# Attention scores of two heads on the two halves of TensorE's rows, three products each, in place of stacked pairs of products; instruction and buffer tables redrawn

## The chip, the cores and the metric

The kernel runs on one core of a Trainium2 chip. The metric is the device time of one execution in microseconds (us); the time before is the median of three runs. Times inside a run come from one profiled execution. The engines are TensorE (PE, with its weight loads shown apart as PEld), VectorE (DVE), ScalarE (ACT), GpSimd (POOL) and SyncE (SP, which here issues transfers).

## The reference

One decoder layer on 512 tokens of width 1024, all in float32: a normalised input is projected to the queries, keys and values of three token mixers and to their gates; the mixers' outputs are gated, added, projected and normalised; a gated feed-forward part follows. The change concerns the scores of two of the mixers (head width 64):

```python
# sliding window with sinks: 8 query heads share 2 key heads, blocks of 128
scores = jnp.einsum('bnqhgd,bnkhd->bnhgqk', qb, kband).astype(jnp.float32) * (d ** -0.5)
scores = jnp.where(mask[None, :, None, None], scores + bias[None, None], -jnp.inf)
...
# stick-breaking: 8 heads, block i of 128 queries against keys up to its end
z = jnp.einsum('bqhd,bkhd->bhqk', q[:, i * BLOCK:L], k[:, :L]).astype(jnp.float32) * (d ** -0.5)
log_1m = jnp.where(causal, jax.nn.log_sigmoid(-z), 0.0)
between = lax.cumsum(log_1m, axis=3, reverse=True) - log_1m
a = jnp.where(causal, jnp.exp(jax.nn.log_sigmoid(z) + between), 0.0)
outs.append(jnp.einsum('bhqk,bkhd->bqhd', a.astype(v.dtype), v[:, :L]))
```

The third mixer attends to 256 memory rows with heads of width 128.

## The kernel before, in words

**Precision.** A float32 operand of most products is held as two parts of the rounded type float32r: `hi`, the rounded value (an ACT cast), and `lo`, the rest (a DVE subtraction). A product is then three matmuls, hi x hi, hi x lo and lo x hi, that add up in one PSUM bank (`mm3`, L455). The transposes and the products of the attention weights with the values take plain float32.

**Tiling.** Weights arrive in blocks of 128x1024 by transfers of 512 KB, are split, and multiply token or feature blocks of 128 rows against up to 512 columns. These dense products (projections, gates, feed-forward) form a stream (`dn`, later `fs`) of units that the attention stages draw from: `dn.run(us)` emits so much dense work between two attention steps.

**Scores before.** A projected block `t` holds two heads of width 64 on its 128 partitions. `proj` (L581) calls for keys `stack_parts` (L553) and for queries `stack_twice` (L564), or the other way round in the window branch. For each head `e` of the two, `stack_parts` puts the head's hi part on 64 partitions and its lo part on the other 64; `stack_twice` puts the hi part on both halves, and in a second tile the lo part on one half above zeros. A matmul over all 128 rows then gives hi x hi + lo x hi at once, so a head's score takes two matmuls and not three. `sb_head` (L1273) does this for the stick-breaking heads one at a time: four blocks of queries against 512, 384, 256 and twice 128 key columns, two matmuls each. `swa_pair` (L1348) does it for two window heads, four blocks of 256 columns each. Two sigmoids (ACT), masks and scans (DVE), ten transposes (PE, against `c_ident`), and products with the values follow. These last (`sb_out`, L1323, and the end of `swa_pair`) already use the array in two halves, by columns: `ys[64 * i : 64 * i + 64, :n]` takes the one head's 64 values on output partitions 0 to 63 and the other's on 64 to 127, 128 rows x 64 columns each, the heads in turn.

**Order.** The program is written stage by stage, but every instruction is recorded per engine (`Noted`, L220) and at the end laid in the order of the tables `ORDER` (L38), one list of instruction numbers for each engine; each instruction is tied behind the one listed ahead of it (L2095). `PLAN` (L148) names for each tile the buffer that it gets; `bank` is the name under which all eight PSUM banks appear, and `pair` that of 28 of the 512-column work tiles, under which many key and query blocks stand. Line numbers of compute instructions in the profile are L232, the recording layer's.

Of the kernel before, what the change touches and what calls it, by code (L numbers as in the profile page):

```python
# [17 lines left out]
P = 128  # L18
D = 1024
S = 512  # L20
# [17 lines left out]
ORDER = {  # L38
    "tensor": (
# [23 lines left out]
    ),  # L63
    "vector": (
# [152 lines left out]
}  # L217


class Noted:  # L220

    def __init__(self, engine):
        self.engine, self.seen = engine, []
# [1965 lines left out]
```

## Time and profile before

| | us |
|---|---|
| median of 3 runs | 768.79 (768.78 to 768.81) |
| the profiled execution, first to last instruction | 766.9 |
| PE busy | 759.1 (99%), 4073 matmul records |
| DVE busy | 675.2 (88%) |
| ACT busy | 520.3 (68%) |
| stick-breaking scores and values on PE | 81.5 to 160.3 of the span |
| window scores and values on PE | 160.3 to 225 of the span |

The span of the profiled execution is 1.9 us shorter than the median. A matmul's record runs from its start to its result, so records of successive matmuls overlap; the pace of PE is read from their starts. A float32 (not float32r) matmul of 64 columns of weights leaves two records in the trace, so that the program's 4009 matmuls are 4073 records. TensorE's granted clock is 1.0 through the run.

### The profile page before, as it was taken

Reading aid. Unit: us, or ns where it says so; the run is one execution under the profiler, and the core shown is the slowest. Engines: PE = TensorE matmul, PEld = TensorE weight load, DVE = VectorE, ACT = ScalarE, POOL = GpSimd, SP = SyncE. Lnnn points to the kernel's source line nnn. Section 1 sums busy time; section 2 is a strip of 40 time slices with the busy share of each in tenths; the row PEclk is TensorE's granted clock in tenths of the full one; section 3 lists DMA queues with packets and bytes.
Section 4 is the critical chain, followed back from the end, with each engine's and each line's share of the span. In section 5 each row is a group of like instructions: output and inputs, shape, how many; then the busy total and the mean of one; then the engine's idle time right before and its main releaser. Section 6 shows DMA issues by size and latency. Waiting matters only on the chain.

```text
span 766.9 us, 11497 instructions
## 1 busy us (share of the span) xinstructions
PE 759.1 (99%) x4073; PEld 647.3 (84%) x4073; DVE 675.2 (88%) x1100; ACT 520.3 (68%) x946; POOL 104.1 (14%) x140
## 2 busy tenths in 40 slices
PE   9999999999999999999999999999999999999996
PEld 6789888778888888888888899988888888888885
DVE  7994897799989756999897799899999999999966
ACT  7662677777997758677944596566666668957552
POOL 0303242000222110010001201100000000214000
PEclk9999999999999999999999999999999999999998
DMA  8548999734799895469949958876777746859922
GB/s 277 166 142 233 332 328 254 211 111 149 185 188 192 184 203 163 112 134 210 340 128 329 209 130 240 203 191 180 204 192 203 220 142 187 171 120 216 261 75 111
DMA packets 50170, 150.06 MB, mean 196 GB/s; under 512 B 5984, under 2 KB 7952, under 8 KB 50016
## 3 DMA queue, kind: packets, MB, share of 16 engines
q1 hardware_dynamic: 34224, 94.38, 36.8%
q0 software_dynamic: 15600, 54.80, 36.1%
q8 instruction: 32, 0.52, 0.3%
q14 instruction: 26, 0.21, 0.1%
q10 hardware_dynamic: 288, 0.13, 0.1%
HBM read 140.38 MB, written 19.40 MB: 208 GB/s over the span
## 4 chain that ended last, share of the span: by engine, by line
PE 96%; DMA 1%; DVE 1%; ACT 1%; issue 0%; SPq 0%; DVEq 0%
PE bank L232 96%; DMA xT<-in_xT 1%; DMA raw<-in_w_p 0%; DVE xacc L232 0%; SPq L232 0%; ACT pair L232 0%; DVE pair L232 0%; ACT hi L232 0%; ACT xT L232 0%; DVE lo L232 0%; DVE fg L232 0%; DVE sl_x L232 0%; DVEq L2180 0%; DVE s L232 0%; ACT sqr L232 0%
## 5 line engine op out<-in xcount | busy, mean ns | idle before, releaser
L232 PE MATMUL bank<-pair,hi 128*128 128x512 f32 (+1 forms) x1008 | 254.4, 368 | 0.0
L232 DVE TENSOR_TENSOR lo<-raw,hi 128x1024 fp32r<-128x1024 f32 (+4 forms) x149 | 170.7, 1149 | 36.8 <-ACT hi L232 36.2
L232 PEld LDWEIGHTS bank<-pair,hi 128*128 128x128 f32 x1008 | 177.5, 189 | 27.0 <-ACT hi L232 0.9
L232 ACT CAST hi<-raw 128x1024 fp32r<-128x1024 f32 (+4 forms) x149 | 147.7, 998 | 73.7 <-PE bank L232 54.5
L232 PE MATMUL bank<-hi,pair 128*128 128x512 f32 (+1 forms) x628 | 196.3, 374 | 0.0
L232 PE MATMUL bank<-pair,lo 128*128 128x256 f32 (+1 forms) x752 | 154.7, 302 | 0.0
L232 PEld LDWEIGHTS bank<-hi,pair 128*128 128x128 f32 x628 | 115.3, 188 | 19.5 <-issue 0.2
L232 PEld LDWEIGHTS bank<-pair,lo 128*128 128x128 f32 x752 | 115.6, 190 | 10.9 <-DVE lo L232 0.7
L232 PE MATMUL bank<-lo,pair 128*128 128x512 f32 (+1 forms) x330 | 123.6, 375 | 0.0
L232 ACT CAST hi<-wide 128x1024 fp32r<-128x1024 f32 (+1 forms) x61 | 62.2, 1024 | 27.0 <-PE bank L232 11.3
L232 DVE TENSOR_TENSOR lo<-wide,hi 128x1024 fp32r<-128x1024 f32 (+1 forms) x61 | 71.9, 1185 | 4.6 <-ACT hi L232 4.3
L232 PEld LDWEIGHTS bank<-lo,pair 128*128 128x128 f32 x330 | 62.0, 188 | 10.1
L232 POOL DMA_DIRECT2D raw<-in_w_g x24 | 21.1, 878 | 124.4 <-DVE lo L232 106.2
L232 DVE TENSOR_TENSOR gp<-gp,bank 128x512 f32<-128x512 f32 x49 | 33.6, 687 | 4.6 <-PE bank L232 3.7
L232 ACT ACTIVATE sg<-gp 128x256 f32<-128x256 f32 x42 | 17.7, 421 | 23.0 <-DVE gp L232 22.9
L232 POOL DMA_DIRECT2D raw<-in_w_gu x15 | 13.2, 924 | 147.6 <-DMA raw<-in_w_gu 138.5
L232 ACT COPY gp<-bank 128x512 f32<-128x512 f32 x42 | 24.7, 588 | 2.1 <-DVE aq L232 1.4
L232 DVE TENSOR_TENSOR_SCAN bw<-br,bw 128x512 f32<-128x512 f32 (+3 forms) x32 | 24.6, 809 | 0.2
L232 DVE TENSOR_TENSOR gp<-gp,hp 128x512 f32<-128x512 f32 x36 | 24.7, 685 | 0.0
L232 POOL DMA_DIRECT2D wide<-in_w_gu x12 | 11.2, 934 | 84.6 <-DMA wide<-in_w_gu 76.3
L232 ACT COPY hp<-bank 128x512 f32<-128x512 f32 x36 | 21.5, 598 | 0.0
L232 PE MATMUL bank<-hi,ll 128*128 128x512 f32 x50 | 19.4, 389 | 0.0
(624 smaller groups left out, 1371.8 us busy)
## 6 DMA issues: line engine op xcount, KB each, us to landing
wide<-in_w_gu SPq DMA_DIRECT2D x31, 512.0 KB, 5.1
raw<-in_w_gu SPq DMA_DIRECT2D x26, 512.0 KB, 5.4
raw<-in_w_g POOLq DMA_DIRECT2D x24, 512.0 KB, 6.0
raw<-in_w_g SPq DMA_DIRECT2D x18, 512.0 KB, 4.2
raw<-in_w_gu POOLq DMA_DIRECT2D x15, 512.0 KB, 7.2
raw<-in_w_p SPq DMA_DIRECT2D x14, 512.0 KB, 6.3
wide<-in_w_gu POOLq DMA_DIRECT2D x12, 512.0 KB, 5.8
raw<-in_w_brt SPq DMA_DIRECT2D x9, 512.0 KB, 4.8
```

Source lines behind the costliest of these rows:

```text
L232: ins = f(*args, **kw)
```

## The change

1. `stack_parts` and `stack_twice` go. Key and query blocks are split like all others, `parts`: one cast on ACT and one subtraction on DVE over 128 partitions, 13 blocks in all. The 26 casts and 26 subtractions on 64 partitions, 10 more casts and 10 memsets fall away.
2. `mm3_rows` computes the scores of two heads with the operands where the projection left them: head 0 on partitions 0 to 63, head 1 on 64 to 127. Each matmul has 64 rows and uses half of the array's rows; there are three of them per score, and the code writes them with the two halves in turn. 128 matmuls of 128 rows go, 192 of 64 rows come, with the same numbers of columns (24 of 512, 24 of 384, 144 of 256).
3. `sb_head` becomes `sb_scores` for two heads and `sb_weights` for one; the stages around are written in another order.
4. Recording is now of the whole program: one table `ORDER` over all engines gives the order in which instructions are put out, and `PLAN` is redrawn with it. Both tables are new from end to end. Fallback code for an empty table goes. ACT loads its function table 12 times and not 9.

```diff
-ORDER = {
-    "tensor": (
...
+ORDER = (
+    "3 1 12 598 15-16 4 13 599-600 18 5 17 6 19 7 20-21 8 23 33 9 22 34 10 24 39-40 11 26 35 25 41 93 37 94 30 42 "
...
-    def stack_parts(kind, idx, t):
-
-        for e in range(2):
-            r, o = 64 * e, 64 - 64 * e
-            x = ck(f"{kind}s{idx}{e}", F32R)
-            nc.scalar.copy(x[r : r + 64, :], t[r : r + 64, :])
...
-    def stack_twice(kind, idx, t):
...
-                with tc.high_priority():
-                    nc.vector.scalar_tensor_tensor(t[:, :], ps[:, :], s, st["rb"][:, :], op0=ALU.mult, op1=ALU.mult)
-                if kind in ("kb", "qa"):
-                    stack_parts(kind, idx, t)
-                elif kind in ("qb", "ka"):
-                    stack_twice(kind, idx, t)
...
+                nc.vector.scalar_tensor_tensor(t[:, :], ps[:, :], s, st["rb"][:, :], op0=ALU.mult, op1=ALU.mult)
+                st[(kind + "s", idx)] = parts(f"{kind}s{idx}", t)
...
-    def sb_head(h):
-        c = h // 2
-        ks, qs, ql = (st[(x, c, h % 2)] for x in ("kbs", "qbs", "qbl"))
...
-            mm(out, qs[:, q], keys, r < 3, False)
-            mm(out, ql[:, q], keys, False, r != 2)
...
+    def mm3_rows(outs, l, r, start):
+
+        for x, y_ in ((0, 0), (1, 0), (0, 1)):
+            for e, out in enumerate(outs):
+                rows = slice(64 * e, 64 * e + 64)
+                mm(out, l[x][rows], r[y_][rows], start and x + y_ == 0, y_ == 1)
+
+    def sb_scores(c):
+        (kh, kl), (qh, ql) = st[("kbs", c)], st[("qbs", c)]
+        z = [[aps(f"z{2 * c + e}{i}") for i in range(3)] for e in range(2)]
...
+            mm3_rows([z[e][i][:, o : o + n] for e in range(2)], (qh[:, q], ql[:, q]), keys, r < 3)
+        for e in range(2):
+            sb_weights(2 * c + e, z[e])
...
-                mm(blocks(s[h], n), qs[:, q], kh, n in (0, 2), False)
-                mm(blocks(s[h], n), qs[:, q], klo, False, True)
...
+            mm3_rows([blocks(s[h], n) for h in hs], q, keys, n in (0, 2))
...
-    for h in range(8):
-        sb_head(h)
...
+    sb_scores(0)
+    dn.run(5.6)
+    for c in range(4):
+        sb_turn(2 * c)
...
+        if c < 3:
+            sb_scores(c + 1)
```

**What the new order does on PE.** Below, before and after, is the order on PE at the scores of the first two stick-breaking heads. Rows name the written tile, the moving operand (keys) and the weights (queries). Before (head 0: `kbs` the stacked keys, `qbs` and `pair_111` the two query tiles):

```order
L232 MATMUL bank_104<-pair_117,lo_82 128x512
L232 MATMUL bank_104<-kbs_316,qbs_409 128x512
L232 MATMUL bank_104<-kbs_316,pair_111 128x512
L232 MATMUL bank_104<-kbs_316,qbs_409 128x384
L232 MATMUL bank_104<-kbs_316,pair_111 128x384
L232 MATMUL bank_104<-kbs_316,qbs_409 128x256
L232 MATMUL bank_104<-kbs_316,pair_111 128x256
L232 MATMUL bank_104<-kbs_316,qbs_409 128x256
L232 MATMUL bank_104<-kbs_316,pair_111 128x256
L232 MATMUL bank_104<-pair_115,hi_78 128x512
```

And after (`kbs0h`, `kbs0l` the keys' hi and lo; `pair_115`, `qbs0l` the queries'; a row reads the same for both halves):

```order
L427 MATMUL bank_101<-kbs0h,pair_115 128x256
L427 MATMUL bank_101<-kbs0h,pair_115 128x512
L427 MATMUL bank_101<-kbs0h,qbs0l 128x512
L427 MATMUL bank_101<-kbs0l,pair_115 128x512
L427 MATMUL bank_101<-kbs0h,pair_115 128x384
L427 MATMUL bank_101<-pair_107,hi_78 128x512 x2
L427 MATMUL bank_101<-pair_107,lo_81 128x512
L427 MATMUL bank_101<-kbs0h,pair_115 128x256
L427 MATMUL bank_101<-kbs0h,qbs0l 128x256
L427 MATMUL bank_101<-kbs0h,pair_115 128x384
L427 MATMUL bank_101<-kbs0h,qbs0l 128x384
L427 MATMUL bank_101<-kbs0l,pair_115 128x384
```

As the code writes them, each of these rows would stand twice in a row, once for each half. In the table's order the three products of one half stand together (the first five rows are all of half 0, the last five of half 1), and dense products over the full array stand between the groups.

The second place is ahead of the scores of heads 2 and 3, where the dense stream and transposes (`c_ident`) run. After the change:

```order
L427 MATMUL bank_101<-pair_109,hi_79 128x512
L427 MATMUL bank_101<-c_ident,bw_880 128x128
L427 MATMUL bank_101<-kbs1h,qbs1h 128x512
L427 MATMUL bank_101<-c_ident,bw_877 128x128 x2
L427 MATMUL bank_101<-c_ident,bw_855 128x128
L427 MATMUL bank_101<-kbs1h,qbs1h 128x256
L427 MATMUL bank_101<-pair_108,lo_83 128x512
```

Single 64-row products have moved in between products of the full array. Before, the score products stood in groups of up to eight, in a few places too with dense products in between, but there all of them used the full array.

The third place is the value products of the first two stick-breaking heads (`at` the transposed weights, `wide` the values; 64 output rows), by column halves in turn. Before:

```order
L232 MATMUL bank_104<-at_1039,wide_84 64x512
L232 MATMUL bank_104<-at_951,wide_84 64x512
L232 MATMUL bank_104<-at_1040,wide_84 64x384
L232 MATMUL bank_104<-at_952,wide_84 64x384
L232 MATMUL bank_104<-at_1041,wide_84 64x256
L232 MATMUL bank_104<-at_953,wide_84 64x256
L232 MATMUL bank_104<-at_1041,wide_84 64x128
L232 MATMUL bank_104<-at_953,wide_84 64x128
```

After:

```order
L427 MATMUL bank_101<-at_1039,wide_84 64x512
L427 MATMUL bank_101<-at_957,wide_84 64x512
L427 MATMUL bank_101<-at_1045,wide_84 64x384
L427 MATMUL bank_101<-at_932,wide_84 64x384
L427 MATMUL bank_101<-at_1036,wide_84 64x256
L427 MATMUL bank_101<-c_ident,bw_1013 128x128
```

The group of eight is cut behind the fifth; the other three stand 28 instructions or so further on. Over the whole program the 8 groups of such products become 22.

More of the change, by code (lines that the diff above doesn't have):

```diff
@@ new lines, with __init__, then, __getitem__ @@
+class View:
+    def __init__(self, make, path=(), shape=None):
+        self.make, self.path, self.shape = make, path, shape
+    def then(self, f):
+        return View(self.make, self.path + (f,))
+    def __getitem__(self, k):
+        return self.then(lambda ap: ap[k])
+    def bitcast(self, dt):
+        return self.then(lambda ap: ap.bitcast(dt))
+    def rearrange(self, *args, **kw):
+        return self.then(lambda ap: ap.rearrange(*args, **kw))
+    def unsqueeze(self, axis):
+        return self.then(lambda ap: ap.unsqueeze(axis))
+    def to_broadcast(self, shape):
+        return self.then(lambda ap: ap.to_broadcast(shape))
+    def real(self):
+        ap = self.make()
+        for f in self.path:
+            ap = f(ap)
+        return ap
@@ new lines, with __init__, put_out @@
+class Op:
+    def __init__(self, at, engine, name, args, kw):
+        self.at, self.engine, self.name, self.args, self.kw = at, engine, name, args, kw
+        self.behind = ()
+class Program:
+    def __init__(self):
+        self.ops = []
+    def put_out(self, nc, order, follow):
+        real = lambda x: x.real() if isinstance(x, View) else x
+        last, out = {}, set()
+        for n in order or range(len(self.ops)):
+            op = self.ops[n]
+            assert all(b.at in out for b in op.behind)
+            out.add(n)
+            args = [real(x) for x in op.args]
+            ins = getattr(getattr(nc, op.engine), op.name)(*args, **{k: real(x) for k, x in op.kw.items()})
+            if op.engine in last:
+                follow(ins, last[op.engine])
+            last[op.engine] = ins
+        assert len(out) == len(self.ops)
@@ L256, in __getitem__, with once, f @@
         return self.held[c]
+def once(make):
+    got = []
+    def f():
+        if not got:
+            got.append(make())
+        return got[0]
+    return f
 class Places:
@@ L456, in mm3 @@
         (lh, ll), (rh, rl) = l, r
-        one = nc.tensor.matmul(out, lh, rh, start=start, stop=False, skip_group_check=True)
+        nc.tensor.matmul(out, lh, rh, start=start, stop=False, skip_group_check=True)
         nc.tensor.matmul(out, lh, rl, start=False, stop=False, skip_group_check=True)
-        return one, nc.tensor.matmul(out, ll, rh, start=False, stop=stop, skip_group_check=True)
-    def mm3_behind(*args):
-        one, last = mm3(*args)
-        if "products" in st:
-            after(one, st["products"])
-        st["products"] = last
+        nc.tensor.matmul(out, ll, rh, start=False, stop=stop, skip_group_check=True)
     def mm(out, l, r, start, stop):
@@ L474, in tile_kernel @@
     pin, since = [], []
-    def after(ins, first):
-        if not ORDER:
-            follow(ins, first)
     def follow(ins, first):
@@ L486, in fn @@
         ins = nc.scalar.activation(*args, **kw)
-        for p in pin:
-            after(ins, p)
+        ins.behind = tuple(pin)
         since.append(ins)
@@ L494, in table, with const @@
         ins = nc.scalar.preload_act_table_set(name)
-        for x in since:
-            after(ins, x)
+        ins.behind = tuple(since)
         since.clear()
         pin[:] = [ins]
-    def const(name, shape, pool=cst):
-        t = places.fixed(cst, shape, F32, f"c_{name}") if pool is cst else pool.tile(shape, F32, name=f"c_{name}")
+    def const(name, shape, pool=None):
+        t = pool.tile(shape, F32, name=f"c_{name}") if pool else places.fixed(shape, f"c_{name}")
         nc.sync.dma_start(t[:, :], a[name])
@@ new lines, in tile_kernel @@
+    idle = tc.nc.const_aps.tensor(1.0, [P, 512], BF16)
+    one_t = {}
+    for name in ("x", "m"):
+        one_t[name] = ck(f"on_{name}", F32R)[:, :P]
+        nc.vector.tensor_copy(one_t[name], idle[:, :P])
+    pw = dps("warm")
+    for i in range(WARM):
+        mm(pw[:, :], idle[:, :P], idle[:, :], True, True)
+    first_load(nc.scalar, 0, (0, 2))
+    first_table = nc.scalar.preload_act_table_set("natural_log_exp_and_others")
+    load_x(0, 1)
+    first_load(nc.sync, 0, (1,))
+    load_x(1, 2)
@@ new lines, in tile_kernel @@
+    first_load(nc.sync, 1, (0, 1))
+    load_x(2, 3)
+    first_load(nc.sync, 1, (2,))
+    first_load(nc.sync, 2, (0,))
+    load_x(3, 4)
+    first_load(nc.sync, 2, (1, 2))
+    load_x(4, 5)
+    first_load(nc.sync, 3)
+    load_x(5, 8)
+    dn.loaded = dn.have = FIRST
+    for p in range(len(PIECE)):
+        for i in range(FIRST):
+            first_split(i, p)
+        for k in range(*PIECE[p]):
+            gain_split(k)
+    xacc = ck("xacc")
+    nc.scalar.activation(xacc[:, :], xraw[0][:, :], AF.Square)
@@ new lines, in tile_kernel @@
+    for k in range(1, KC):
+        nc.scalar.activation(xraw[k][:, :], xraw[k][:, :], AF.Square)
+        nc.vector.tensor_tensor(xacc[:, :], xacc[:, :], xraw[k][:, :], op=ALU.add)
+    dn.ahead(4, 3)
+    for i in range(FIRST):
+        first_ps[("kb", i)] = aps(f"kb{i}")
+    order = [(i, 0, x) for x in ("hh", "lh", "hl") for i in range(FIRST)]
+    order += [(i, 1, x) for i in range(FIRST) for x in ("hh", "lh", "hl")]
+    for i, k, x in order:
+        w = (his if x[0] == "h" else los)[i]
+        mm(first_ps[("kb", i)][:, :], w[:, k * P : (k + 1) * P], u[k][x[1] == "l"], k == 0 and x == "hh", False)
@@ L2065, in tile_kernel @@
     kept(1)
-    behind(since[-1], st["mixed"])
     table("silu_and_others")
@@ L2083, in tile_kernel @@
     for t in (2, 3):
-        late = turn_late(t, 0)
-    behind(*late)
+        turn_late(t, 0)
     fs.hold = 10
@@ L2094, in tile_kernel @@
     go(len(fs.units))
-    for e, text in ORDER.items():
-        seen, last = getattr(nc, e).seen, None
-        for part in text.split():
-            a, _, b = part.partition("-")
-            for k in range(int(a), int(b or a) + 1):
-                if last is not None:
-                    follow(seen[k], seen[last])
-                last = k
+    order = []
+    for part in ORDER.split():
+        a, _, b = part.partition("-")
+        order += range(int(a), int(b or a) + 1)
+    program.put_out(tc.nc, order, follow)
 def _buckets():
```

401 lines of the change are left out of this document (144 added, 257 removed), and 427 rows, old and new, of tables (ORDER, PLAN).

## The prediction

> **What bounds the kernel now.** I read the page's busy times first, then the chain of waits, then the busy times by stage, and last the order in time on TensorE (PE) in the stages that the change touches.
>
> ```profile
> PE 759.1 (99%) x4073; PEld 647.3 (84%) x4073; DVE 675.2 (88%) x1100; ACT 520.3 (68%) x946; POOL 104.1 (14%) x140
> PE 96%; DMA 1%; DVE 1%; ACT 1%; issue 0%; SPq 0%; DVEq 0%
> 22.29 737.97 PE bank L232 x3990
> 22.30:80.00 57.70, 57.70 (x322) 52.54 (x323) 45.36 (x71) 28.85 (x44) 15.59 (x29) 1.00 0.65 185
> 80.00:160.00 80.00, 80.00 (x477) 66.22 (x477) 68.22 (x110) 58.93 (x112) 18.21 (x28) 1.00 0.91 272
> 160.00:225.00 65.00, 65.00 (x379) 53.57 (x376) 61.53 (x173) 55.39 (x144) 9.03 (x11) 1.00 0.61 158
> 760.30:767.00 6.70, 0.00 (x0) 0.00 (x0) 2.46 (x6) 1.17 (x4) 0.00 (x0) 0.68 0.42 157
> ```
>
> The third row is the chain in order of time: from 22.29 us to the end of the last product it is one unbroken piece of 738 us on PE. The last four rows are stages; after the stage's length come PE, PE's weight loads, DVE, ACT and POOL. PE is busy in every microsecond of each stage but the tail, while DVE has 11.8 us left of 80 and ACT 21.1 in the stage with the stick-breaking scores (80 to 160 us). A matmul's record includes its latency, so "busy" alone doesn't prove that PE is at its pace. A far stretch gives the pace:
>
> ```profile
> 560.37 2.00 PE L232 MATMUL bank<-pair,hi 128*128 128x512 f32 x8
> 562.21 1.11 PE L232 MATMUL bank<-pair,lo 128*128 128x256 f32 x8
> 563.16 2.00 PE L232 MATMUL bank<-pair,hi 128*128 128x512 f32 x8
> ```
>
> Eight products of 512 columns take 562.21 - 560.37 = 1.84 us, 0.23 each; eight of 256 take 0.95, 0.12 each. The stage of the scores runs at the same pace, as the eight products of head 0 show:
>
> ```profile
> 81.53 0.40 PE L232 MATMUL bank<-kbs,qbs 128*128 128x512 f32 x1
> 81.76 0.39 PE L232 MATMUL bank<-kbs,pair 128*128 128x512 f32 x1
> 81.99 0.33 PE L232 MATMUL bank<-kbs,qbs 128*128 128x384 f32 x1
> 82.16 0.34 PE L232 MATMUL bank<-kbs,pair 128*128 128x384 f32 x1
> 82.33 0.28 PE L232 MATMUL bank<-kbs,qbs 128*128 128x256 f32 x1
> 82.45 0.28 PE L232 MATMUL bank<-kbs,pair 128*128 128x256 f32 x1
> 82.57 0.28 PE L232 MATMUL bank<-kbs,qbs 128*128 128x256 f32 x1
> 82.69 0.29 PE L232 MATMUL bank<-kbs,pair 128*128 128x256 f32 x1
> 82.82 0.63 PE L232 MATMUL bank<-pair,hi 128*128 128x512 f32 x2
> ```
>
> They start 0.23, 0.17 and 0.12 us apart and the next work follows at once. So PE is the bound everywhere: what the change adds to PE's stream lengthens the run one for one, and work taken from DVE, ACT or POOL is worth nothing.
>
> **What is taken off the other engines.** The stacked splits ran on 64 partitions:
>
> ```profile
> L232 DVE TENSOR_TENSOR kbs<-kb,kbs 64x512 fp32r<-64x512 f32 x5 | 3.4, 685 | 0.1
> L232 DVE CAST qbs<-qb 64x512 fp32r<-64x512 f32 x5 | 2.1, 423 | 0.1
> L232 ACT CAST kbs<-kb x5: 611/618/629, 29.3 to 36.3; 64x512 fp32r<-64x512 f32 x5
> L232 DVE TENSOR_TENSOR mT<-mT,mT 128x512 f32<-128x512 f32 x3 | 2.1, 686 | 0.0
> L232 ACT ACT_TABLE_LOAD x9 | 11.5, 1283 | 1.8 <-PEq L2174 1.7
> ```
>
> DVE loses 26 subtractions (0.685) and 10 casts (0.423) and gets 13 subtractions of 128x512 (0.686): 22.0 - 8.9 = 13 us less. ACT loses 26 casts of 0.618 for 13 (at about the same 0.62) and gets three table loads of 1.28: 4 us less. POOL loses 10 memsets. All of it lies beside a PE that doesn't wait: 0 us.
>
> **Products: between +3.4 and +9.0 us.** Removed are 128 products: per head 512, 384, 256 and 256 columns twice (0.23 + 0.17 + 0.12 + 0.12, twice: 1.28 us, eight heads 10.2), and 64 window products of 256 (7.7): 17.9 us. Added are 192 of 64 rows with the same columns, three for each two. If two heads' halves always ran side by side, that would be 13.5 us. But the redrawn order doesn't let the halves alternate: I count 42 separate groups of 64-row products, 14 of them a single product, in which the half changes only 25 times from one product to the next. One after another they take 26.9 us (+9.0). If a product may start only when the one ahead of it has started, a change of half hides one product: 24.1 (+6.2). If each half runs down its own part of a group, however long, the groups take 21.3 (+3.4). The nearest row for the overlap is the one place where the kernel already uses halves, the value products, by columns:
>
> ```profile
> 121.83 0.39 PE L232 MATMUL bank<-hi,ml 128*128 128x512 f32 x1
> 122.15 2.38 PE L232 MATMUL bank<-at,wide 128*64 128x512 f32 x16
> 124.46 0.50 PE L232 MATMUL bank<-hi,mh 128*128 128x512 f32 x1
> 124.79 0.40 PE L232 MATMUL bank<-lo,mh 128*128 128x512 f32 x1
> 122.15 0.20 PEld L232 LDWEIGHTS bank<-at,wide 128*64 128x64 f32 x4 [0.35 <-ACT yq L232]
> 122.64 0.14 PEld L232 LDWEIGHTS bank<-at,wide 128*64 128x64 f32 x2 [0.29 <-issue]
> 123.06 0.14 PEld L232 LDWEIGHTS bank<-at,wide 128*64 128x64 f32 x2 [0.28 <-issue]
> 123.39 0.14 PEld L232 LDWEIGHTS bank<-at,wide 128*64 128x64 f32 x2 [0.18 <-issue]
> 123.71 0.57 PEld L232 LDWEIGHTS bank<-at,wide 128*64 128x64 f32 x6 [0.18 <-issue]
> L232 PE MATMUL bank<-at,wide x64: 272/432/643, 109.1 to 160.1; 128*64 128x512 f32 x16, 128*64 128x384 f32 x16, 128*64 128x256 f32 x16, 128*64 128x128 f32 x16
> L232 PE MATMUL bank<-pts,wide x64: 272/379/430, 175.4 to 223.9; 128*64 128x256 f32 x48, 128*64 128x128 f32 x16
> ```
>
> These are eight products that alternate between the halves, each in two records (float32). The weight loads come two by two, 0.42 us apart for 512 columns: one record of each half at a time, though both records of the first half stand ahead of the second half's. So a product of the other half overtakes one that waits, by at least one place. With one place the 64-row groups take 22.9 us, without limit 21.3. I take 22.1, **+4.2 us**.
>
> The Trainium skill ("TensorE: Matmul & The Clock Gate", Part 3, "The mechanism") says that matmuls keep strict order in start and end, which would give the 24.1 instead (+6.2). The rows of the column halves speak against it here.
>
> **Value products, by columns: +3.8 us.** The change doesn't edit them, but the redrawn order cuts their 8 groups (8 products each, halves alternating) into 22, seven with one product alone. Per product: 0.85 us for 512 columns (two records of 0.42), 0.64 for 384 (two of 0.32, from 123.06 to 123.39 and 123.71), and in proportion 0.43 and 0.22. A group lasts as long as its longer half: 4 x 2.13 + 4 x 1.51 = 14.6 us before, 18.4 after by the same sum. The floor is this sum, since it lets the halves overtake without limit; with no overlap lost it would be 0.
>
> **Changes of the array's split: +17.9 us, the unknown.** The last group of rows prices a change. Into the column halves: the first starts 0.32 us after a 512-column product that otherwise takes 0.23 (+0.09), and its own slot is 0.49 (122.15 to 122.64) against 0.42 (+0.06, the load that wasn't hidden): 0.15. Back: the last pairs are two of 256 and two of 128 from 123.71 on, 0.65 us, so 124.36, and the next starts at 124.46 (+0.10) and lasts 0.33 instead of 0.23 (+0.10): 0.20. A full round is 0.35. Before there are 16 changes. In the new order I count 109: 22 into columns and 87 into row halves or back to the full array. No row here shows a row half. The bounds are 0 for a change between rows and full array (then only the 14 more column groups cost, 14 x 0.35 = 4.9 us), and the column price for all, with 0.20 for whatever loads 128 columns of weights: 14 x 0.15 + 79 x 0.20 = 17.9 us. I take the upper end: the column split is the only row near it, and nothing in the trace tells why rows should do without.
>
> "TensorEngine Tiling (Array Packing)" of the Trainium skill, "Key Properties", says that changing the mode, not merely the tile, drains TensorE; the trace agrees for columns (0.09 and 0.10 us), and for rows no run here shows it yet.
>
> **Waits and the new order: 0.** Behind the first 22 us PE has one idle gap that its records show:
>
> ```profile
> 22.29 0.50 PE L232 MATMUL bank<-sl_x,on_x 128*128 128x512 f32 x1 [0.37 <-DVE sl_x L232]
> ```
>
> So a better order can win 0.4 us. A worse one can make PE wait; the engine with the least room is DVE from 160 to 225 us, with 65.00 - 61.53 = 3.5 us. A longer PE stream leaves it more. I take 0, from -0.4 to +3.5.
>
> Sum: 4.2 + 3.8 + 17.9 = +25.9 us on the execution's 766.9 us: 792.8. The median lies 1.9 above that execution (768.79): **794.7, say 794 us**.
>
> **Rivals.**
> - *Row halves change for nothing.* Then 4.2 + 3.8 + 4.9 = +12.9: 781.7 us. For it: the full array and its transposes (same size) follow each other without a gap, and only the column split shows one. Against: the column price has two parts, and the late weight load is not peculiar to columns.
> - *No overtaking and the full price.* +6.2 to +9.0 instead of +4.2: 797 to 800 us. Against it: the paired loads above.
> - *The halves really run side by side, so not slower.* The place is the 64-row groups: PE would have to hold back a half's products across the full products between two groups, so that each product costs half its columns, 13.5 us instead of 17.9 (-4.4), with the changes of split free of charge and columns back at 14.6. Then 768.8 - 4.4 = 764 us; with the cut column groups (+3.8) 768, no difference. It decides once a 64-row product costs under about half of a full one and a change under 0.02 us. Against it: the 0.09 us gaps, and that groups of one product have nothing beside them. "TensorEngine Tiling", "Theoretical Speedup", promises up to twice for 64 rows; it speaks of filled tiles, which this order doesn't give.
> - *A new wait becomes the bound*: where the new order puts a product just behind the DVE operation that frees its bank, PE idles. One such operation of 0.69 us at each of the 16 heads is 11 us: 806. For it only the 3.5 us of room; against it that DVE loses 13 us of work.
>
> **Chances.** Forecast (full price, 786 to 799) 0.60; free row changes (777 to 786) 0.20; no overtaking 0.08; side by side 0.07; a new wait above 802 0.05. The range 778 to 802 leaves out the last two and a little of the second. A measurement of this kernel tells 0.2% (1.5 us) from no change; the side-by-side case splits into 0.05 faster and 0.02 same, a small part of the first rival (0.01) adds to same, all else is slower: 0.05 faster, 0.03 same, 0.92 slower.
>
> **What would show it.** In the profile after: PE still at 99% and alone on the chain; records of 64 rows; a single 64-row product among full ones starting about 0.32 us after a 512-column product rather than 0.23, with the product behind it late by 0.2; three 64-row products of one half 0.23 apart at 512 columns; pairs of starts a few ns apart only where the half changes. If full products follow 64-row ones without a gap, the 17.9 is wrong by 13; if starts of different halves interleave over long groups, the 4.2 is at its low end; idle time of PE with a releaser would be the last rival.

## The result and the profile after

The changed kernel takes **836.50 us** (median of 4 runs, 835.05 to 837.78) against 768.78: a ratio of 1.0882, 95% interval 1.0867 to 1.0898, or +67.7 us. Forecast were 794 us, 778 to 802. The sign was right, the size short by 42 us. The profiled execution spans 835.0 us, 68.1 more than the 766.9 before.

From the page of the kernel after, the busy times and the chain by engine:

```profile
PE 801.3 (96%) x4137; PEld 650.2 (78%) x4137; DVE 668.1 (80%) x1077; ACT 520.2 (62%) x936; POOL 100.0 (12%) x130
PE 86%; ACT 5%; DMA 4%; DVE 3%; issue 1%; DVEq 0%; ACTq 0%
```

PE's records now cover 96% of the span and not 99%: 33.7 us without any. Its share of the chain fell from 96% to 86%, and ACT's rose from 1% to 5%, though ACT works no longer than before (520 us). So PE waits, and for ACT more than for others. The same kernel by stages (columns as in the prediction's windows):

```profile
80.00:160.00 80.00, 79.34 (x430) 58.37 (x429) 59.56 (x95) 51.03 (x94) 13.48 (x20) 1.00 0.63 186
160.00:225.00 65.00, 62.92 (x330) 43.63 (x329) 38.98 (x97) 35.89 (x85) 0.00 (x0) 1.00 0.34 106
500.00:600.00 100.00, 93.65 (x581) 82.53 (x581) 87.33 (x114) 58.22 (x88) 8.73 (x10) 1.00 0.70 186
600.00:700.00 100.00, 91.25 (x505) 77.63 (x504) 85.75 (x110) 54.41 (x79) 6.11 (x7) 1.00 0.60 153
```

The largest holes are from 500 to 700 us. That is the feed-forward part: no score is computed there, and the change edits none of its operations; it only takes ties of order (`behind`) out of that code. What is new there are the tables of the order and of the buffers. The waits of PE, by the tile of the operation that ended them (total us, times, longest):

```profile
PE bank L427 <- ACT hp L427: 16.2, 25, 0.7
PE bank L427 <- ACT yq L427: 2.9, 6, 0.5
```

`hp` is a copy in the feed-forward part. A unit there has 16 products into two neighbouring banks. Eight take the hi weights and write 512 columns, `main` (256) and `rest` (256). Then eight take the lo weights and write `main` alone. ACT copies `main` to `gp` and `rest` to `hp`. The copy of `rest` needs only the eight hi products. The order in time after the change, PE and the copies:

```profile
630.01 2.23 PE L427 MATMUL bank<-pair,hi 128*128 128x512 f32 x9
632.08 0.40 PE L427 MATMUL bank<-pair,lo 128*128 128x256 f32 x2
632.51 0.58 ACT L427 COPY hp<-bank 128x512 f32<-128x512 f32 x1 [0.39 <-PE bank L427]
633.15 0.97 PE L427 MATMUL bank<-pair,lo 128*128 128x256 f32 x6 [0.68 <-ACT hp L427]
```

The new order puts `hp` behind the second lo product. The copy waits until those two are through, and the third lo product starts 0.06 us after the copy's end. The two products start at 632.08 and take 0.24 at their pace, so PE could have gone on at 632.32; it went on at 633.15, 0.83 us later. Yet the copy reads none of the columns that the lo products write. Before, both copies stand behind all 16 products, and the next unit runs in other banks meanwhile. The same place of the kernel before:

```profile
506.34 1.12 PE L232 MATMUL bank<-pair,lo 128*128 128x256 f32 x8
507.29 2.00 PE L232 MATMUL bank<-pair,hi 128*128 128x512 f32 x8
...
507.50 0.59 ACT L232 COPY gp<-bank 128x512 f32<-128x512 f32 x1
507.98 0.59 ACT L232 COPY hp<-bank 128x512 f32<-128x512 f32 x1
```

The wait is written in the program. Of the 256-column products with lo weights (`pair,lo`), none carries a wait on ACT in the program before, and 34 do after: 32 wait for an `hp` copy, 2 for a gate function (`sg`), each of which reads other columns of the bank that the product writes. Over all matmuls the count hardly moves, 237 before and 239 after; it has to be taken by group of products.

**How much waiting there is in all.** A record of a product runs past its slot, so idle time in the records counts less than what is lost. I therefore summed, over the places behind the first 22 us and outside the two stages of the scores (80 to 225 us) where a full-array product follows a full-array product, the distance of their starts beyond the pace (0.227 us for 512 columns, 0.120 for 256). Below this is called the dense excess; it is worked out from the trace's starts, by my own sum. Before it is 3.3 us, after 37.7: 10.1 from 500 to 600 us, 13.0 from 600 to 700, 5.8 from 300 to 400, 8.8 elsewhere. So of the +68.1 us, 34.4 are waits outside the scores.

**The price of a change of split**, the other large term, reads as forecast. A single 64-row product among full ones, after the change:

```profile
95.41 0.62 PE L427 MATMUL bank<-pair,hi 128*128 128x512 f32 x2
95.96 0.49 PE L427 MATMUL bank<-kbs1h,qbs1l 64*128 64x512 f32 x1
96.39 0.50 PE L427 MATMUL bank<-pair,lo 128*128 128x512 f32 x1
96.72 0.60 PE L427 MATMUL bank<-c_ident,bw 128*128 128x128 f32 x4
```

The second of the two products at 95.41 starts 0.23 later, at 95.64. The 64-row product starts 0.32 behind that (+0.09), holds PE for 0.43 in place of 0.23 (+0.20), and the next one for 0.33 (+0.10). That is 0.39 us for two changes, 0.20 each. The whole program fits: the 42 groups of 64-row products last 31.3 us from first start to the next product's start, which is the forecast's 22.1, 0.8 of waits inside groups and 0.20 for each group. The other 0.19 of a round lies in the products on both sides.

### The profile page after: what moved, and what is told of

It is laid out like the page before. It is cut to its first block, busy times and chain, and to the rows that moved or that the text cites. A ratio compares the mean times of both kernels' runs of the same rounds, so it can differ in the third digit from the quotient of the medians.

```text
span 835.0 us, 11634 instructions
## 1 busy us (share of the span) xinstructions
PE 801.3 (96%) x4137; PEld 650.2 (78%) x4137; DVE 668.1 (80%) x1077; ACT 520.2 (62%) x936; POOL 100.0 (12%) x130
## 4 chain that ended last, share of the span: by engine, by line
PE 86%; ACT 5%; DMA 4%; DVE 3%; issue 1%; DVEq 0%; ACTq 0%
PE bank L427 86%; DMA raw<-in_w_g 2%; ACT hp L427 2%; DMA raw<-in_w_brt 1%; ACT hi L427 1%; DVE lo L427 1%; ACT yq L427 0%; ACT pair L427 0%; DVE fg L427 0%; DMA raw<-in_w_p 0%; DVE s L427 0%; DVE gp L427 0%; DVE wide L427 0%; ACT sg L427 0%; ACT sqr L427 0%
## 5 line engine op out<-in xcount | busy, mean ns | idle before, releaser
L427 PE MATMUL bank<-pair,hi 128*128 128x512 f32 (+1 forms) x1056 | 271.8, 367 | 0.6 <-ACT hi L427 0.3
L427 PE MATMUL bank<-hi,pair 128*128 128x512 f32 (+1 forms) x810 | 245.3, 380 | 2.3 <-ACT gq0p L427 1.3
L427 PE MATMUL bank<-pair,lo 128*128 128x256 f32 (+1 forms) x784 | 175.3, 306 | 17.1 <-ACT hp L427 16.2
L427 PEld LDWEIGHTS bank<-hi,pair 128*128 128x128 f32 x810 | 148.9, 188 | 32.9 <-ACT gq1p L427 1.9
L427 PE MATMUL bank<-lo,pair 128*128 128x512 f32 (+1 forms) x426 | 157.8, 379 | 0.0
L427 PEld LDWEIGHTS bank<-pair,lo 128*128 128x128 f32 x784 | 125.5, 189 | 37.0 <-ACT hp L427 22.5
L427 PEld LDWEIGHTS bank<-lo,pair 128*128 128x128 f32 x426 | 79.6, 188 | 15.0 <-DVE lo L427 1.5
L427 PE MATMUL bank<-pair,pair 128*128 128x512 f32 (+3 forms) x216 | 55.4, 362 | 0.6 <-DVE s L427 0.6
L427 PEld LDWEIGHTS bank<-pair,pair 128*128 128x128 f32 (+1 forms) x216 | 34.9, 187 | 10.6 <-issue 3.9
L427 POOL DMA_DIRECT2D raw<-in_w_g x24 | 22.1, 920 | 105.9 <-DVE lo L427 48.6
L427 DVE TENSOR_TENSOR_SCAN bw<-br,bw 128x384 f32<-128x384 f32 (+3 forms) x32 | 24.8, 811 | 0.5 <-ACT br L427 0.2
```

The source lines that it names most:

```text
L427: ins = getattr(getattr(nc, op.engine), op.name)(*args, **{k: real(x) for k, x in op.kw.items()})
```

## Experiments

The theories. A: products and changes of split cost what the prediction says, and the rest comes from the order tables, above all from the place of the `hp` copies. B: what is missing comes from the 64-row products themselves or from changes that cost more in company. The kernel before ran beside every experiment, at 768.5 to 768.9 us. The expectations letter their own cases, each explained where it stands; their block-sparse heads are the stick-breaking ones. Of an edit of the tables one place is shown.

### The change without its order

The changed program in the order and buffers of the kernel before (tables `ORDER` and `PLAN`); the scores of each head stand where that kernel has them, so the halves hardly alternate:

```diff
 ORDER = (
-    "3 1 12 598 15-16 4 13 599-600 18 5 17 6 19 7 20-21 8 23 33 9 22 34 10 24 39-40 11 26 35 25 41 93 37 94 30 42 "
+    "1-32 40 33 35 37 74 48 42 44 50 46 52 89 186-188 607 0 39 41 34 36 38 49 43 45 51 47 53 75 58 54 56 60 62 "
...
```

> The changed kernel's program (three products of 64 rows, blocks split once) with the kernel before's order on every engine and its buffers, as far as they match; the scores of each head stand where the kernel before has them. Only the redrawn tables are undone. Theory A (the 37.7 us that the full-array products wait in the changed kernel, 3.3 before, come from the redrawn order, and a change of the array's split costs 0.20 us): 768.8 + products 24.5 - 17.9 = +6.6 + 38 more changes (54 against 16) x 0.20 = +7.6, together 783 us (778 to 788), PE without idle time. Theory B (the waits belong to the new products and splits themselves, whatever the order): still above 810. Theory C (row halves change for nothing, the score part of the changed kernel is long because of waits): 768.8 + 6.6 = 775.

Measured: **783.30 us** (783.29 to 783.52), ratio 1.0189 [1.0174, 1.0205]. From its page, its waits of PE, and its windows:

```profile
PE 773.7 (99%) x4137; PEld 655.0 (84%) x4137; DVE 662.3 (85%) x1077; ACT 513.3 (66%) x933; POOL 98.7 (13%) x130
```

```profile
PE bank L306 <- PEq L2174: 0.8, 1, 0.8
PE bank L306 <- DVE sl_x L306: 0.6, 1, 0.6
```

```profile
160.00:225.00 65.00, 65.00 (x373) 51.27 (x373) 57.17 (x149) 48.30 (x119) 4.51 (x5) 1.00 0.48 133
500.00:600.00 100.00, 100.00 (x580) 88.23 (x579) 93.84 (x120) 65.31 (x99) 8.73 (x10) 1.00 0.73 189
```

With the old order the change costs 14.5 us, as A of the expectation has it (783), and the two waits are those of the kernel before (1.2 us there, 1.4 here). The other 53 us belong to the tables: to the waits that they make, and to the 55 more changes of split and the cut groups of value products.

The same with 128 rows in each score product. This program's scores mix two heads: each product sums over both heads' rows.

```diff
-                rows = slice(64 * e, 64 * e + 64)
+                rows = slice(0, 128)
```

> As the run with the kernel before's order, but each of the three products takes all 128 rows instead of its 64, so no row halves are left (the scores then mix two heads, the output isn't the reference's). Products one after another 26.9 - 17.9 = +9.0, changes 16 as before: A and C 777.8 us (776 to 780). So A says 5 us less than with row halves (38 changes x 0.20 less 2.4 us of overlap), C says 2 to 3 us more than with them. B: above 810 here too.

Measured: **777.96 us** (777.86 to 778.62), 1.0122 [1.0105, 1.0139]. There are 64 products more and the splits are those of before: +9.2 us, where the prediction has +9.0 for 192 products one after another (26.9 for 17.9). The 64-row form then adds 5.3: 38 more changes at 0.20 are 7.6, less some overlap where the half changes.

### The new order without 64-row products

The same edit on the changed kernel, with its own tables (this program's scores mix two heads too).

> The changed kernel with its own order and buffers, but each of the three products takes all 128 rows (the scores then mix two heads, the output isn't the reference's): 44 changes of the array's split instead of 109, nothing overtakes. A: 836.5 + 4.8 (products) - 65 x 0.20 = 828 us (824 to 831), the waits of the full-array products as they are. C: 836.5 + 4.8 = 841. If the waits were caused by the row halves' lost time rather than by the order, they would go too: below 800.

Measured: **828.74 us** (826.73 to 829.75), 1.0777 [1.076, 1.0794]. Its waits of PE:

```profile
PE bank L427 <- ACT hp L427: 16.2, 25, 0.7
PE bank L427 <- ACT yq L427: 2.9, 6, 0.5
```

The row of `hp` is the same to the digit, and the dense excess is 37.9 us. Without one 64-row product nearly the whole loss remains: theory B falls.

### Which part of the new order

The tables were joined from two halves. First before's order up to the first feed-forward product (product 2254 of 4073), the new order behind it:

```diff
 ORDER = (
-    "3 1 12 598 15-16 4 13 599-600 18 5 17 6 19 7 ...
+    "1-32 40 33 35 37 74 48 42 44 50 46 52 89 186-188 607 0 ...
...
```

> The kernel before's order and buffers up to the first feed-forward product (product 2254 of 4073), the redrawn order and buffers behind it, as far as they fit (161 of 1676 tiles lie elsewhere). No score product is in the redrawn part. A: 783.3 + the 28.5 us that full-array products wait behind 400 us in the changed kernel = 812 us (806 to 816). If the waits came from lost time at the scores: 783 to 786.

Measured: **815.24 us** (813.85 to 815.55), 1.0599 [1.0584, 1.0615]. Its waits:

```profile
PE bank L364 <- ACT hp L364: 16.1, 25, 0.7
PE bank L364 <- DVE mt L364: 2.8, 1, 2.8
```

That is 31.9 us over the old order throughout (783.3), or 29 without the single wait for `mt`, which ends at 455.5 us, where the two orders meet. Then the other way round: new up to product 1900, the old one behind; 107 tiles had to get other buffers.

> The reverse: the redrawn order and buffers up to product 1900 (the scores and all attention), the kernel before's order and buffers behind it (107 tiles lie elsewhere, which may cost some waits where the two meet). A: 836.5 - 28.5 - part of the 5.8 us of 300 to 400 us = 804, plus up to 15 us where the buffers had to be moved: 804 to 820. If the waits came from the scores: 834 and more.

Measured: **818.26 us** (817.06 to 819.74), 1.0643 [1.0627, 1.0659]. Its waits and a window:

```profile
PE bank L357 <- DVE gp L357: 7.1, 1, 7.1
PE bank L357 <- ACT yq L357: 2.9, 6, 0.5
```

```profile
500.00:600.00 100.00, 100.00 (x634) 90.75 (x633) 93.93 (x125) 62.59 (x97) 9.60 (x11) 1.00 0.77 205
```

From 500 to 600 us PE is full again and the wait for `hp` is gone from the list. The 7.1 us are one wait that ends at 701 us, some 300 us behind the place where the two orders meet; the moved buffers are a likely reason, but no run separates them. Without it the run would be near 811. So the feed-forward order is worth some 25 to 32 us, and what lies ahead of it the rest, score products and changes included.

### The copies

To put the suspect into a kernel that has no other fault: the old order of the first experiment, and each of the 36 `hp` copies put out behind the second of its unit's eight 256-column products, as the new order has it.

```diff
-    ... 4010 4007 4012-4027 4031 4028-4029 4033-4034 ...
+    ... 4010 4007 4012-4021 4029 4022-4027 4031 4028 4033-4034 ...
```

(4012 to 4027 are a unit's products, 4028 is `gp`, 4029 is `hp`.)

> The run with the kernel before's order (783.3 us, PE without waits), with one thing of the redrawn order put in: each of the 36 copies of a wide bank's second columns (hp<-bank), there behind all 16 products of its step, is emitted behind the second of the eight 256-column products instead, as the redrawn order has it 32 times. The copy reads none of the columns that the products behind it write. Theory A1 (a product that is emitted behind a copy waits for the copy wherever both touch the same bank): PE drains at each copy, about 0.39 + 0.58 + 0.06 us less little, 36 times about 1.1: 783.3 + 40 = 823 us (813 to 829). Theory A2 (only columns that overlap make a wait, the redrawn order waits for other reasons): ACT's new order costs a little: 783 to 791.

Measured: **827.63 us** (826.25 to 829.12), 1.0764 [1.0748, 1.0781]. Its waits:

```profile
PE bank L309 <- ACT hp L309: 32.5, 35, 3.2
```

36 copies, moved and nothing else, cost 44.3 us, 1.2 each on average: A1 holds, A2 is out. By the starts of the products on both sides, 25 of the copies cost 0.83 to 0.88 us, as in the changed kernel. Ten cost 1.24 to 3.34: they start 0.4 to 2.5 us after the two products are through, nine of them because ACT is still at other work.

Then the reverse, in the changed kernel:

```diff
-    ... 4017 4059 4018-4021 4029 4022-4025 4062 4026 4082 4027 ...
+    ... 4017 4059 4018-4024 4029 4025 4062 4026 4082 4027 ...
```

> The changed kernel with its own buffers and order, only the 32 early copies (hp<-bank) are moved behind the last product of their step. If the early copies alone cause the waits of 500 to 700 us (23.1 us): about 836.5 - 23 = 813. If the order also leaves too little work between a step's last product and the next product into its bank (0.84 to 2.6 us for 28 of the 42 copies gp<-bank, by the products' starts, where the kernel before has 2.78 or more), the copies then end later than that work and nothing is won: 836 to 846.

Measured: **841.13 us** (840.66 to 842.47), 1.0944 [1.0925, 1.0962]. Its waits of PE and the order in time:

```profile
PE bank L428 <- ACT hp L428: 21.2, 31, 1.3
```

```profile
637.37 0.75 PE L428 MATMUL bank<-pair,lo 128*128 128x256 f32 x5
638.16 0.58 ACT L428 COPY hp<-bank 128x512 f32<-128x512 f32 x1 [1.61 <-PE bank L428]
638.80 0.62 PE L428 MATMUL bank<-pair,lo 128*128 128x256 f32 x3 [0.68 <-ACT hp L428]
```

The time agrees with the rival in the expectation, but the rows say otherwise. Contrary to the text on record, the edit put the 32 copies behind the fifth of the eight products, not the last; three products into the bank still follow and wait as before. The run decides nothing about a copy behind the last product. It does show that moving a copy by three places within its unit doesn't help. The edit was then made in full, each copy directly behind `gp`:

```diff
-    ... 4018-4021 4029 4022-4025 4062 4026 4082 4027 4083-4084 4095-4097 4028 4098 ...
+    ... 4018-4025 4062 4026 4082 4027 4083-4084 4095-4097 4028-4029 4098 ...
```

> The changed kernel with its own order and buffers, and only this moved: each of 35 copies of a feed-forward unit's rest columns (hp) is put out directly behind the copy of its main columns (gp), so behind all 16 products of its unit, as in the kernel before. An earlier run that was meant to do this moved 32 of the copies only from behind the second to behind the fifth of the unit's eight 256-column products; three products of the same bank still stood behind each. Theory A (a product waits for any copy out of its bank that is put out ahead of it; the copies' place is the largest single cause of the waits): the waits on these copies, some 25 times 0.8 us, go; what stays are waits where the units are interleaved and the next product into the bank comes soon: 819 us, 810 to 824, and the row of PE waiting for hp falls from 16.2 us to under 8. Theory B (the interleaved units leave too little time between a unit's last product and the next product into its bank, so the wait only moves to there): 832 to 840. Theory C (all of the dense stretches' 34 us hang on these copies): 802.

Measured: **816.70 us** (815.95 to 817.29), 1.0627 [1.0609, 1.0644], 19.8 us less than the changed kernel. Its waits of PE, and two windows:

```profile
PE bank L426 <- ACT yq L426: 2.9, 6, 0.5
PE bank L426 <- ACT hp L426: 1.2, 5, 0.3
```

```profile
500.00:600.00 100.00, 98.45 (x614) 87.64 (x613) 92.41 (x121) 59.45 (x90) 9.62 (x11) 1.00 0.72 195
600.00:700.00 100.00, 99.39 (x563) 86.29 (x562) 94.02 (x124) 66.51 (x102) 6.14 (x7) 1.00 0.63 171
```

The wait for `hp` falls from 16.2 to 1.2 us and the dense excess from 37.7 to 17.4, by 20.3. So 20 of the 34 us of waits outside the scores are the place of 35 copies: theory A. The 256-column products with lo weights that carry a wait on ACT fall from 34 to 2, the two for `sg`. Theory C of the expectation (all 34 us) is out: 14 us stay, spread over many small waits.

### Halves side by side

Could the 64-row products pay for themselves without the new order? In the old order, the heads of six pairs were brought together where the second head stood, the two halves in turn:

```diff
-    ... 646-650 652 654 656 658 660 662 ... 651 653 655 657 659 661 ...
+    ... 748-750 650-654 674-676 683 ...
```

> As the run with the kernel before's order, but the products of a pair's two heads stand together at the second head's place, the halves alternating, for six of the eight pairs (the other two found no free banks): products 17.8 instead of 24.5 us if each half runs beside the other, changes 51 instead of 54. A: 783 - 6.7 - 0.6 = 776 us (772 to 780). If halves do not run side by side in a group: 783 to 786.

Measured: **801.64 us** (800.07 to 802.26), 1.0424 [1.0409, 1.044], a miss by 26 us. Its waits:

```profile
PE bank L300 <- DVE bw L300: 14.7, 6, 2.8
```

The first head's scores now come later, and with them its scans on DVE; its transposes stand where they stood, and PE waits there for the scan's result `bw`, six times. Next, only the window heads together, and then (last) three stick-breaking pairs too, at the first head's place and with the second head's work moved along:

```diff
-    "1387 1389 1391 1393 1395 1397 1399 1401 1403 1405 1407 1409 1388 1390 1392 1394 1396 1398 1400 1402 1404
+    "1387-1411 1413-1414 1412 1415 1420 1419 1418 1417 1416 1427 1429-1430 1428 1431 1379 1421-1424 1346-1357
```

> The changed program in the order and buffers of the kernel before, as in the run with that order, but in the sliding-window part the score products of the two heads of a pair stand together and alternate between the halves; the block-sparse heads keep their own places. Theory (halves run side by side where they alternate, a change of split is 0.20 us, and nothing is gained or lost by waits because the second head's transposes keep their distance): 45 changes instead of 54, -1.8 us; in alternating groups the 64-row products take 21.2 us instead of 26.3, -5.1 us; 783.3 - 6.9 = 776.4 us, 775 to 778. Rival (bringing two heads together always buys a wait, as with six pairs where the waits of PE were 25 us): 783 us or more, with a row of PE waiting for DVE or ACT in the score part. Rival (halves are not run side by side): 781.5 us.

Measured: **781.37 us** (781.01 to 781.66), 1.0163 [1.0149, 1.0176]: 1.9 us under the old order, not 6.9. That is the number of the rival "halves are not run side by side" (781.5), yet the rows of the groups show that this rival is wrong and that its number came about by chance. One of the groups in time, and a window:

```profile
183.38 0.39 PE L301 MATMUL bank<-pair,qas1h 64*128 64x256 f32 x2
183.60 0.28 PE L301 MATMUL bank<-pair,qas1l 64*128 64x256 f32 x2
183.72 0.40 PE L301 MATMUL bank<-pair,qas1h 64*128 64x256 f32 x4
...
184.80 0.28 PE L301 MATMUL bank<-pair,qas1h 64*128 64x256 f32 x2
```

```profile
160.00:225.00 65.00, 62.98 (x394) 49.05 (x393) 57.82 (x157) 48.66 (x120) 6.76 (x8) 1.00 0.51 139
```

The halves do run side by side: 24 products of 256 columns start between 183.38 and 184.80, two at a time, 0.12 us a pair. With 0.2 for the last pair that is 1.62 us, where 24 in a row at 0.12 would take 2.9. Over all groups of 64-row products, from first start to the next full product, that is 24.9 us and 29.7 in the old order: 4.8 saved. I had expected 6.9, since I counted the old order's groups (26.3) as if one product were hidden at each turn of the half. The rows of the old order's run show about three. This group there has six products of one half and then nine of the other:

```profile
184.69 0.38 PE L306 MATMUL bank<-pair,qas1h 64*128 64x256 f32 x1
184.91 0.28 PE L306 MATMUL bank<-pair,qas1l 64*128 64x256 f32 x1
185.03 0.40 PE L306 MATMUL bank<-pair,qas1h 64*128 64x256 f32 x3
185.26 0.29 PE L306 MATMUL bank<-pair,qas1l 64*128 64x256 f32 x2
...
186.29 1.73 PE L306 MATMUL bank<-pts,wide 128*64 128x256 f32 x16
```

The row at 185.03 holds three products in the 0.23 us up to the next row, where three in a row would take 0.36. Two of them start 7 ns apart: the third of the first half and the first of the second, ahead of three that the program puts out before it. The group lasts 1.60 us; less 0.19 for its end that is 1.41, where 15 in a row at 0.12 would take 1.80, and 1.68 if each had to start behind the one ahead of it. And in the run with the window pairs 2.0 us of PE's time in this stage (65.00 less 62.98) became waits.

```diff
-    "... 606 621 636-643 646-650 652 654 656 ... 745 651 653 655 657 659 661 ...
+    "... 606 621 636-643 646-674 677 675-676 680 678 ... 745 687 690 ...
```

> As the run with the sliding-window pairs, and three of the block-sparse pairs brought together too, each where the first head stood, with the second head's chain of work moved with it, so that 12 groups of 64-row products are left, 35 changes of split instead of 54. Without waits: changes -3.8 us, products 15.4 us instead of 26.3, -10.9 us: 783.3 - 14.7 = 768.6 us, level with the kernel before (768.8). With waits as the order of the operations lets one foresee them, some 2 to 4 us in the score part: 771 to 773 us. Rival (each pair brought together buys more wait than its alternation saves): above 776 us. Faster than the kernel before by over 0.2% (below 767.3) would need side-by-side products to be worth more than the 0.120 and 0.227 us each that the trace shows.

Measured: **774.36 us** (774.19 to 774.57), 1.0071 [1.0059, 1.0084]. Its page:

```profile
PE 762.6 (99%) x4137; PEld 645.6 (84%) x4137; DVE 661.4 (86%) x1077; ACT 512.1 (66%) x933; POOL 98.7 (13%) x130
```

This is 1.4 us above the expected 771 to 773, and below the rival's 776. It is the best version of the change that was run, 62 us under the changed kernel and still 5.5 slower than the kernel before. The groups now take 18.8 us with the slots lost at their ends, nearly the 17.9 of the 128 products they replace. So three half-array products for two full ones only about break even when nearly all alternate, and what is left of the loss is the changes of split around them and some 2 us more of idle PE (772.7 - 762.6 = 10.1 us of the span, 7.8 before).

## Why the prediction was wrong

- **What bounds the kernel (PE alone): right before, no longer after.** The prediction expected PE at 99% and alone on the chain. It is at 96% and 86%.
- **Other engines, 0 us: right.** DVE has 7 us less work (675.2 to 668.1; 13 were forecast, and with the old order it is 662.3) and ACT the same (4 less were forecast), and neither appears in the time.
- **Products +4.2, changes of split +17.9: right.** A change to or from row halves costs 0.20 us; the 42 groups' 31.3 us in the changed kernel fit the forecast's 22.1 with this price; the bound of 0 and the rival "row halves change for nothing" are out. With the old order the same prices give 38 x 0.20 = 7.6 and some 7 for products one after another with turns, 14.6 in all; measured are 14.5. Halves overtake at a turn of the half, by about three products where one was the least assumed.
- **The rivals "no overtaking" and "side by side": both out for this order.** Of the first, the group of six and nine is the proof, since a product of the second half starts there ahead of three of the first. Alternating groups decide nothing here, for they would run side by side without any overtaking too. The Trainium skill ("TensorE: Matmul & The Clock Gate", Part 3, "The mechanism") has matmuls in strict order of start and end; the starts at 185.03 don't fit that for products of different halves. "TensorEngine Tiling (Array Packing)", "Key Properties", says that a change of mode drains TensorE; that agrees, now for rows too, with the 0.09 and 0.10 us above.
- **Value products +3.8: too small, in part by the same kind of wait.** From first start to the next product's start, the 8 groups take 15.9 us before and the 22 take 27.0 after, with 64-row products or without. Of these +11.1, the forecast has 6.0: the 3.8, and 0.16 (0.06 + 0.10) for the part of each of the 14 more rounds that falls inside. Of the other 5.1, 2.9 are the row of PE waiting for `yq`: six times a copy out of the other columns of the group's bank is put out inside the group, as here:

```profile
141.31 0.86 PE L427 MATMUL bank<-at,wide 128*64 128x256 f32 x6
142.63 0.43 PE L427 MATMUL bank<-at,wide 128*64 128x128 f32 x2 [0.46 <-ACT yq L427]
```

- **"Waits and the new order: 0": the step that failed.** The prediction took the span behind 22 us, saw 0.4 us of idle time, and bounded a worse order by +3.5, which is DVE's room in one stage of the scores. But the tables were new from end to end, and I looked for their effect only in the stages of the scores. They put 34 feed-forward products behind an ACT read of other columns of their own bank and cost 34.4 us outside the scores, 20 of them by the `hp` copies.
- **The rival "a new wait becomes the bound": the right kind, in the wrong place, too small, at 0.05.** It named DVE at the 16 heads and 806 us; it was above all ACT at the 36 feed-forward units, and 836. What could have shown it was at hand in the built programs: 256-column products with lo weights and a wait on ACT, 0 before and 34 after, beside the trace's rows of ACT's copies (0.59 us, twice behind eight products).

The accounting of the +68.1 us: forecast terms 25.9; dense excess 34.4 (20.3 the `hp` copies, 14.1 small waits that no run takes apart); the remaining 7.8 are 5.1 at the value products, of them 2.9 waits for `yq`, 1.4 behind the last product (8.5 us from its start to the end of the span, 7.1 before), and 1.3 that stay open.

Why the products wait for a copy of other columns: what is shown is that the programs hold that wait, and what it costs. Taking it away while copy and products still share a bank wasn't tried. The Trainium skill ("PSUM — Partial Sum Buffer", "PSUM bank collisions raise a hardware error") gives a reason: two engines may not touch one bank and quadrant of partitions at once, disjoint columns included, so accesses are to be guarded by bank and not by address. The waits agree with that; no run here shows a collision.

## What to carry to other kernels

A redrawn order is an edit of every stage: compare, between the two built programs and group by group, which instructions of the bottleneck engine carry a wait on another engine, in the stages whose operations the change leaves alone too. Read a PSUM bank out behind its last product; an "early" copy of finished columns stops the next product into the same bank, here mostly for 0.84 us. Three half-array products for two full ones came near to breaking even only in long groups that alternate between the halves, since each change of the array's split costs 0.20 us, about a 512-column product.

## What the runs showed of the hardware that was not expected

- Halves of the array take turns so tightly that 24 products of 64 rows and 256 columns pass in 1.62 us, 0.067 us each, against 0.120 one after another.
- Row halves cost about as much as column halves: 0.39 us for the two changes around a single product, where the trace before gives 0.35 for columns.
- At a turn of the half in a long run, about three products of the second half run beside the last three of the first: 15 products of 256 columns in 1.41 us and not 1.80.
- ACT starts a copy of 512 columns before the record of the one ahead of it ends: 507.50 and 507.98, 0.48 apart, with records of 0.59 us each.
